# Moving the SBUF operands of a hybrid encoder layer from 64 and 192 to 0 modulo 256 bytes

## The chip, the cores and the metric

The kernel runs on one core of a Trainium2 chip. The metric is device time in microseconds, the median of three runs. Addresses in this document are byte offsets within a partition of SBUF, and the **phase** of an operand is the address of its first byte modulo 256.

## The reference, cut to what matters

One layer on 1,024 tokens of width 1,024, all in float32. `u = RMSNorm(x) @ W_in`; half of the columns go through a gated causal depthwise convolution of 31 taps, LayerNorm and swish; the others through chunk-causal retention with 4 heads of 128, per-head RMSNorm and a swish gate. Then

```python
x = x + concat([a_out, b_out], axis=-1) @ w_out     # 1024 x 1024
h = rms_norm(x, norm2_g)
x = x + square(relu(h @ w_ff1)) @ w_ff2              # 1024 x 4096 and 4096 x 1024
return rms_norm(x, final_g)
```

Neither the kernel before nor the change alters what is computed.

## The kernel before

**Matmuls.** A float32 product is made of three matmuls of type float32r, with both factors split into a high part and a low rest: `mm3` (L134 to L138) issues high by high (L136), high by low (L137) and low by high (L138) into one PSUM bank. The stationary operand (`lhsT`) is 128 columns of 4 bytes, the moving operand (`rhs`) 512 columns of 4 bytes (256 in four calls at the very end). Each matmul is preceded by the load of its stationary operand, which runs beside the matmul before it. There are 1,418 calls of `mm3`, so 4,254 such matmuls; 371 plain float32 ones (transposes, retention) come on top. In the rows the first name after the arrow is the moving operand and the second the stationary one.

**Stages, in the order of time.** Input projections and convolution (`acc<-cols,w` and `acc<-w,cols`), retention, the out-projection of the retention half and then of the convolution half (`out_proj`, L484; stationary `mh`, `ml`; 16 calls of 24 matmuls), the columns of the normed result (`normed_columns`, L605), the first feed-forward product, the second one (`ff2_group`, L845; `acc<-w,w` shown as `acc<-w`) and the last norm and stores. The first feed-forward product takes one pair of hidden blocks plainly (`plain_pair`, L727: `acc<-h,w1h`, 96 matmuls) and 15 pairs by Strassen's scheme with seven products of 12 matmuls each (`strassen_pair`, L741: M1, M2, M6, M5, M7, M3, M4, in that order; M1 and M2 are `pa<-h,w1h` and `pb<-h,w1h`). Between the plain pair and the first Strassen pair's third product stand sums of the stashed columns, which come back from DRAM (`bf`, L803, and the operations on VectorE and ScalarE from L806 to L820).

**Where the tiles lie.** Pools take their room one behind the other, in the order of L56 to L65, and a tile's slot is rounded up to 32 bytes. Every tile that a matmul reads begins at its slot's start plus a multiple of 512 bytes, so the slot decides the phase:

| pool | slots x bytes (before) | first address, phase before | phases of the slots before | phases after |
|---|---|---|---|---|
| `const` (ones, vectors, eight `r1` of 4 bytes) | small | 16,512 | mixed | mixed, 64 bytes shorter |
| `blkp` (`blk`) | 8 x 4,096 | 18,496, phase 64 | 64 | 0 |
| `wp` (`w`, `cols`, `h2`, `t`, `bf`, `w2raw`) | 13 x 8,192 | 51,264, phase 64 | 64 | 0 |
| `rawp` (`raw`, `xr` of the second product) | 2 x 4,096 | 157,760, phase 64 | 64 | 0 |
| `cp` (tag "c": `xcol`, `glu`, `y`, `xn`, `w1h`, `w1l`, `t12`, `t34`, `ysum`) | 7 x 4,224 | 165,952, phase 64 | 64, 192, 64, 192, 64, 192, 64 | 0 |
| `sp` (tag "s": `mh`, `ml`, `a22`, `hid`, `part`, `kT`, `qT`, `xr` of L504) | 11 x 2,048 | 195,520, phase 192 | 192 | 0 |
| `hx` (`tx`, the low part for M7) | 1 x 8,192 | 220,096, phase 192 | 192 | 0 |

The length of a `cp` slot comes from its longest tile, `glu` (L270): 30 columns of padding and 1,024 of data, 4,216 bytes, rounded to 4,224, which is 16 x 256 + 128. The slots of `cp` are handed out in turn, so from pair to pair the high and low parts of W1 (`w1h`, `w1l`, made in `split_pairs`, L667) come to lie at phase 64 or 192. Of the 4,254 float32r matmuls 3,150 have both operands at phase 64, 1,044 a moving operand at 64 and a stationary one at 192, 36 the reverse, and 24 both at 192.

For example, in the pair whose product M1 starts at 521.79 us, the four operands of M1 and M2 lie in slots of phase 192; in the pair whose M1 starts at 560.67 us they lie in slots of phase 64.

Of the kernel before, what the change touches and what calls it, by code (L numbers as in the profile page):

```python
# [8 lines left out]
F32 = mybir.dt.float32  # L9
# [6 lines left out]
P = 128  # L16
D = 1024
S = 1024
# [3 lines left out]
PAD = KT - 1  # L22
# [8 lines left out]
GB = 2  # L31
NG = NB // GB
WARM = 11
QUOTA = (4, 16, 11, 11, 13, 33, 22, 14)
NPAIR = NF // 2

# [2 lines left out]
def hybrid_layer_kernel(  # L39
# [16 lines left out]
    const = pool("const", 1)  # L56
# [3 lines left out]
    cp = pool("cp", 7)  # L60
# [87 lines left out]
    def mean_sq(src):  # L148

        tr = sp.tile([P, D], BF16, tag="s", name="trash")  # L150
        ss = tiny.tile([P, 1], F32, tag="ss1", name="ss")
        nc.scalar.activation(tr, src, AF.Square, scale=D**-0.5, accum_out=ss)
        return ss
# [60 lines left out]
                proj_tokens(w, b, a, d, d == 0, d == ND - 1)  # L214
        return accs

    r1 = {}

    def evac_v(b, acc):
        nc.vector.scalar_tensor_tensor(  # L220
# [18 lines left out]

    def stats(t):  # L240

        xt = cp.tile([P, D], F32, tag="c", name="xt")
        nc.sync.dma_start(xt, x[t * P : (t + 1) * P, :])
        r1[t] = const.tile([P, 1], F32, name=f"r1_{t}")
        m = tiny.tile([P, 1], F32, tag="nmr", name="m1")
        nc.gpsimd.tensor_tensor(m, mean_sq(xt), eps1, ALU.add)
        nc.gpsimd.tensor_tensor(r1[t], m, mhalf[:, 0:1], ALU.pow)
# [19 lines left out]
    glu, marks = [], []  # L267

    def glu_gate(accs):
        g = cp.tile([P, PAD + S], F32, tag="c", name="glu")  # L270
        nc.gpsimd.memset(g[:, 0:PAD], 0.0)
        for h in range(2):
            zg = sp.tile([P, HALF], F32, tag="s", name="zg")
            nc.vector.tensor_tensor(zg, accs[1][h], r1_row[h], ALU.mult)
            sg = sp.tile([P, HALF], F32, tag="s", name="sg")
            nc.scalar.activation(sg, zg, AF.Sigmoid)
            sr = sp.tile([P, HALF], F32, tag="s", name="sr")
            nc.gpsimd.tensor_tensor(sr, sg, r1_row[h], ALU.mult)
            nc.vector.tensor_tensor(g[:, PAD + h * HALF : PAD + (h + 1) * HALF], accs[0][h], sr, ALU.mult)
        glu.append(g)  # L280
        marks.append(len(pe_log))
# [17 lines left out]
    with tc.manual_schedule(engines=ordered):  # L299

        idle = pr.tile([P, 4, P], F32, tag="r", name="idle")
        for i in range(WARM):
            nc.tensor.matmul(idle[:, i % 4], lhsT=ones, rhs=ones, start=True, stop=True)
# [12 lines left out]
    for t in range(NB):  # L316
        stats(t)
# [16 lines left out]
    nc.sync.dma_start(trg, trig)  # L334

    glu_gate(first)
    wv = chunk_w(0)
    for q in range(2):
        accs[q].append(bank(1))
    for d in range(ND):  # L340
        glu_proj(w, 1, accs, d, 1)
    glu_gate(accs)

    def glu_tile(w, j):
# [14 lines left out]
    for j in range(2):  # L359
        if j == 1:  # L360
            wk = chunk_w(3)
        glu_gate(glu_tile(w, j))
# [213 lines left out]
    i = 0  # L576
    for (a, b), n in zip(zip(marks, marks[1:]), QUOTA):
        for j in range(n):
# [441 lines left out]
```

## Time and profile before

| | |
|---|---|
| median of 3 runs | 1077.8 us (1075.88 to 1078.59) |
| the profiled execution | 1076.53 us |
| its span, first to last instruction | 1074.8 us |
| mean granted TensorE clock | 0.991 |
| TensorE busy | 1039.7 us, 97% of the span |
| VectorE, ScalarE, GpSimd busy | 803.4, 381.5, 69.4 us |
| HBM | 125 GB/s over the span |

The profiled execution is 1.73 us longer than its span; that is launch and end, which no row shows. Busy time of TensorE counts each matmul to its modelled end, so neighbours overlap: what a matmul costs in a dense stretch is the distance from its start to the next one's, not its duration.

### The profile page before, as it was taken

The numbers are of one execution on the slowest core, as the hardware profiler recorded it, in microseconds if no ns is written. First come the engines' busy times: TensorE is split into PE (matmuls) and PEld (weight loads), VectorE is DVE, ScalarE is ACT, GpSimd is POOL, SyncE is SP. The second block draws the span as 40 slices with busy tenths as digits, with TensorE's granted clock in tenths as the row PEclk, the third lists the DMA queues.
The fourth block names the chain that finished last, engine by engine and source line by source line (L and its number), as shares of the span: only waits on it lengthen the run. The fifth ranks groups of instructions, "written<-read, shape, count | busy, mean of one in ns | idle before, by whom it ended". The sixth has DMA issues, their size and how long they took to land.

```text
span 1074.8 us, 12628 instructions
## 1 busy us (share of the span) xinstructions
PE 1039.7 (97%) x4772; PEld 856.7 (80%) x4772; DVE 803.4 (75%) x975; ACT 381.5 (35%) x601; POOL 69.4 (6%) x134
## 2 busy tenths in 40 slices
PE   9999999999999989969999999999999999999996
PEld 7888888888888777748888888887788888888885
DVE  5397769999796455687677676776998878777857
ACT  7511111144531465333232332322453333433423
POOL 0400110021000311000000000000000000000003
PEclk9999999999999999979999999999999999999998
DMA  9412011002241024615334444356546344253324
GB/s 357 166 40 79 26 53 59 21 14 66 92 140 63 1 59 155 219 68 176 138 135 169 138 161 138 133 185 213 199 143 250 117 176 164 95 186 103 92 78 156
DMA packets 55020, 134.88 MB, mean 126 GB/s; under 512 B 5424, under 2 KB 13744, under 8 KB 54576
## 3 DMA queue, kind: packets, MB, share of 16 engines
q1 hardware_dynamic: 54960, 134.09, 36.4%
q8 instruction: 37, 0.61, 0.2%
q14 instruction: 23, 0.19, 0.1%
HBM read 97.11 MB, written 36.96 MB: 125 GB/s over the span
## 4 chain that ended last, share of the span: by engine, by line
PE 52%; DVE 2%; DMA 1%; issue 1%; POOL 1%; ACT 0%; SPq 0%; POOLq 0%; DVEq 0%; ACTq 0%
PE acc L136 9%; PE acc L138 9%; PE acc L137 9%; PE pa L138 5%; PE pa L137 5%; PE pa L136 5%; PE pb L138 4%; PE pb L137 4%; PE pb L136 4%; DMA xr<-x1M 1%; DVE ot L917 0%; DMA w2raw<-in_w_dram 0%; DVE blk L909 0%; ACT trash L936 0%; POOL var L938 0%
## 5 line engine op out<-in xcount | busy, mean ns | idle before, releaser
L136 PE MATMUL acc<-w 128*128 128x512 f32 x454 | 176.8, 389 | 0.8 <-ACT w L187 0.8
L137 PE MATMUL acc<-w 128*128 128x512 f32 x454 | 176.2, 388 | 0.0
L138 PE MATMUL acc<-w 128*128 128x512 f32 x454 | 175.9, 388 | 0.0
L373 DVE SCALAR_TENSOR_TENSOR y<-glu,vec,y 128x1024 f32<-128x1024 f32 x120 | 153.7, 1290 | 2.0
L136 PEld LDWEIGHTS acc<-w 128*128 128x128 f32 x454 | 85.2, 188 | 19.8 <-ACT w L187 1.3
L136 PE MATMUL acc<-w,cols 128*128 128x512 f32 x256 | 100.1, 391 | 0.0
L137 PE MATMUL acc<-w,cols 128*128 128x512 f32 x256 | 99.8, 390 | 0.0
L138 PE MATMUL acc<-w,cols 128*128 128x512 f32 x256 | 99.8, 390 | 0.0
L137 PEld LDWEIGHTS acc<-w 128*128 128x128 f32 x454 | 85.2, 188 | 17.6
L138 PEld LDWEIGHTS acc<-w 128*128 128x128 f32 x454 | 85.2, 188 | 17.6
L187 ACT ACTIVATE w<-xr 128x1024 fp32r<-128x1024 f32 (+1 forms) x56 | 56.2, 1004 | 105.5 <-PE acc L138 57.4
L188 DVE TENSOR_TENSOR w<-xr,w 128x1024 fp32r<-128x1024 f32 (+1 forms) x56 | 64.7, 1155 | 27.9 <-ACT w L187 27.8
L889 DVE TENSOR_TENSOR blk<-acc,blk 128x512 f32<-128x512 f32 x112 | 72.7, 686 | 11.8 <-PE acc L138 11.6
L113 ACT ACTIVATE w<-raw 128x1024 fp32r<-128x1024 f32 (+1 forms) x36 | 34.8, 966 | 96.9 <-PE acc L138 71.6
L136 PE MATMUL pa<-t,w1h 128*128 128x512 f32 x120 | 47.9, 399 | 10.0 <-ACT part L751 10.0
L138 PEld LDWEIGHTS acc<-w,cols 128*128 128x128 f32 x256 | 48.1, 188 | 9.8
L137 PEld LDWEIGHTS acc<-w,cols 128*128 128x128 f32 x256 | 48.1, 188 | 9.8
L136 PEld LDWEIGHTS acc<-w,cols 128*128 128x128 f32 x256 | 48.1, 188 | 9.8
L136 PE MATMUL acc<-w,mh 128*128 128x512 f32 x128 | 52.0, 406 | 0.0
L187 ACT ACTIVATE w1h<-t 128x1024 fp32r<-128x1024 f32 x30 | 31.7, 1057 | 55.9 <-PE pb L138 55.9
L136 PE MATMUL acc<-cols,w 128*128 128x512 f32 x128 | 50.0, 392 | 1.1 <-ACT w L113 0.9
L137 PE MATMUL acc<-w,mh 128*128 128x512 f32 x128 | 50.7, 396 | 0.0
(193 smaller groups left out, 2094.6 us busy)
## 6 DMA issues: line engine op xcount, KB each, us to landing
raw<-in_w_dram SPq DMA_DIRECT2D x34, 512.0 KB, 3.6
w2raw<-in_w_dram SPq DMA_DIRECT2D x30, 512.0 KB, 4.5
raw<-in_w_in_dram SPq DMA_DIRECT2D x23, 512.0 KB, 3.3
xt<-in_x_dram SPq DMA_DIRECT2D x8, 512.0 KB, 9.0
raw<-in_w_out_dram SPq DMA_DIRECT2D x8, 512.0 KB, 3.3
xr<-in_x_dram SPq DMA_DIRECT2D x16, 256.0 KB, 3.0
stash<-full SPq DMA_DIRECT2D x16, 256.0 KB, 2.6
out_dram<-ot SPq DMA_DIRECT2D x16, 256.0 KB, 2.0
```

What stands on the lines that cost most here:

```text
L113: nc.scalar.activation(w[:, 0, i], raw[:, i], AF.Copy)
L136: nc.tensor.matmul(acc, lhsT=lh, rhs=rh, start=first, stop=False, **kw)
L137: nc.tensor.matmul(acc, lhsT=lh, rhs=rl, start=False, stop=False, **kw)
L138: pe_log.append(nc.tensor.matmul(acc, lhsT=ll, rhs=rh, start=False, stop=last, **kw))
L187: nc.scalar.activation(hi, src, AF.Copy)
L188: nc.vector.tensor_tensor(lo, src, hi.bitcast(F32), ALU.subtract)
L373: nc.vector.scalar_tensor_tensor(y, glu[c][:, k : k + S], tap(k), y, ALU.mult, ALU.add)
L889: nc.vector.tensor_tensor(t, acc[lane][r], t, ALU.add)
```

## The change

The tile `glu` becomes 4,352 bytes long (17 x 256), and with it each slot of `cp`. The eight `r1` tiles of the constants pool become six tiles of 8 bytes: tokens 0 and 1 share one, tokens 2 and 3 another. That frees two slots of 32 bytes, so `const` ends at 18,432 instead of 18,496, and every later pool begins 64 bytes further down. Together all operands of the 4,254 float32r matmuls come to lie at phase 0. `ones`, `ident`, `mhalf` and `vec` stay where they are.

```diff
+ALIGN = 256
...
-    r1 = {}
+    r1, r1_pair = {}, None
...
     def stats(t):
 
+        nonlocal r1_pair
         xt = cp.tile([P, D], F32, tag="c", name="xt")
         nc.sync.dma_start(xt, x[t * P : (t + 1) * P, :])
-        r1[t] = const.tile([P, 1], F32, name=f"r1_{t}")
+        if t % 2 == 0 or t >= 4:
+            r1_pair = const.tile([P, 2], F32, name=f"r1_{t}")
+            r1[t] = r1_pair[:, 0:1]
+        else:
+            r1[t] = r1_pair[:, 1:2]
...
     def glu_gate(accs):
-        g = cp.tile([P, PAD + S], F32, tag="c", name="glu")
+        g = cp.tile([P, S + ALIGN // 4], F32, tag="c", name="glu")
```

The instructions of all five engines, their order, their sizes and what each waits for are the same in both kernels; addresses alone differ, and two of the eight `r1` are now the second column of their tile.

## Rows read from the trace of the kernel before

**Rows 1.** The page's first part: busy time, share of the span, instructions
```profile
PE 1039.7 (97%) x4772; PEld 856.7 (80%) x4772; DVE 803.4 (75%) x975; ACT 381.5 (35%) x601; POOL 69.4 (6%) x134
```

**Rows 2.** Waits of TensorE: waiting instruction, releaser, total us, times, longest
```profile
PE pa L136 <- ACT part L751: 10.0, 1, 10.0
PE pt L617 <- DVE xn L608: 6.7, 8, 1.2
PE pa L138 <- DVE w1l L188: 2.3, 1, 2.3
```

**Rows 3.** Windows: stretch, its us, engines' busy us (x count), clock, DMA share, GB/s
```profile
474.50:751.80 277.30, 277.30 (x1201) 225.70 (x1200) 196.07 (x267) 83.84 (x114) 0.00 (x0) 1.00 0.45 156
763.00:1046.00 283.00, 283.00 (x1249) 233.97 (x1248) 225.16 (x255) 107.11 (x113) 0.19 (x1) 1.00 0.42 141
```

**Rows 4.** Timeline of TensorE, M1 and M2, slots at 192: start, duration
```profile
521.79 0.40 PE L136 MATMUL pa<-h,w1h 128*128 128x512 f32 x1
...
527.38 0.40 PE L136 MATMUL pa<-t,w1h 128*128 128x512 f32 x1
```

**Rows 5.** The same two products of a later pair, slots at 64
```profile
560.67 0.39 PE L136 MATMUL pa<-h,w1h 128*128 128x512 f32 x1
...
566.12 0.40 PE L136 MATMUL pa<-t,w1h 128*128 128x512 f32 x1
```

**Rows 6.** Timeline of TensorE, an out-projection of the retention half
```profile
314.63 0.39 PE L137 MATMUL acc<-w,mh 128*128 128x512 f32 x1
...
319.76 0.40 PE L138 MATMUL acc<-w,ml 128*128 128x512 f32 x1
```

**Rows 7.** Timeline of TensorE, half an out-projection of the convolution half
```profile
395.53 0.39 PE L137 MATMUL acc<-w,mh 128*128 128x512 f32 x1
...
397.84 0.39 PE L138 MATMUL acc<-w,ml 128*128 128x512 f32 x1
```

**Rows 8.** Timeline of TensorE, the plain pair
```profile
433.07 0.40 PE L136 MATMUL acc<-h,w1h 128*128 128x512 f32 x1
...
448.33 0.40 PE L137 MATMUL acc<-h,w1h 128*128 128x512 f32 x1
```

**Rows 9.** Timeline of TensorE, a piece of the last block, 256 columns wide
```profile
1064.14 0.28 PE L138 MATMUL acc<-w 128*128 128x256 f32 x1
...
1064.50 0.28 PE L138 MATMUL acc<-w 128*128 128x256 f32 x1
```

**Rows 10.** VectorE, ScalarE by tile `w1l`, `w1h`: ns min/median/max, first and last start
```profile
L188 DVE TENSOR_TENSOR w1l<-t,w1h x30: 1215/1219/1227, 467.3 to 734.4; 128x1024 fp32r<-128x1024 f32 x30
...
L187 ACT ACTIVATE w1h<-t x30: 1045/1056/1065, 449.6 to 732.8; 128x1024 fp32r<-128x1024 f32 x30
```

**Rows 11.** Timeline: TensorE behind its long wait
```profile
465.05 0.80 PE L136 MATMUL pa<-t,w1h 128*128 128x512 f32 x1 [10.01 <-ACT part L751]
...
469.15 0.63 PE L136 MATMUL pa<-t,w1h 128*128 128x512 f32 x1
469.58 0.63 PE L137 MATMUL pa<-t,w1h 128*128 128x512 f32 x1
...
471.69 0.40 PE L136 MATMUL pa<-t,w1h 128*128 128x512 f32 x1
```

**Rows 12.** The chain that ended last, 739 to 762 us: start, us, what
```profile
743.08 5.07 DMA w2raw<-in_w_dram
...
755.32 5.39 DMA xr<-x1M
...
761.84 0.50 PE acc L136
```

**Rows 13.** DMA issues by line: count, KB each, median us to landing
```profile
xr<-in_x_dram SPq DMA_DIRECT2D x16, 256.0 KB, 3.0
...
bf<-stash SPq DMA_DIRECT2D x3, 1024.0 KB, 5.8
...
xr<-x7M SPq DMA_DIRECT2D x7, 256.0 KB, 2.7
```

## The prediction

> **What bounds the kernel now.** I read the page's busy times first: TensorE is busy for 97% of the span [rows 1]. Next the waits of TensorE: beside one of 10.0 us, one of 2.3 us and eight short ones of 6.7 us together there is little [rows 2], so nearly all of the time is the matmuls following one another. Their own durations are modelled and overlap, so the third view is that of windows in which TensorE never pauses: the stretch divided by the count is what one matmul costs. In the second feed-forward product this is 283.00 / 1249 = 226.6 ns, in the Strassen pairs 277.30 / 1201 = 230.9 ns [rows 3], for the same matmul of 512 columns at the same granted clock of 1.00 (2.4 GHz).
>
> The fourth view is the timeline of two spots that differ in nothing but where the stationary operands lie. M1 and M2 of one pair, with their W1 parts in slots of phase 192, take 5.59 us for 24 starts, 232.9 ns each [rows 4]. The same two products of a later pair, with the parts in slots of phase 64, take 5.45 us, 227.1 ns each [rows 5]. Lines, moving tiles, pool and the work of the other engines are the same. So a float32r matmul whose two operands have different phases costs some 6 ns more than one whose operands agree. VectorE and ScalarE show nothing of the kind: their passes over the same rotating slots last 1215 to 1227 and 1045 to 1065 ns [rows 10], with not 2% between the shortest and the longest.
>
> Whether the sum of the phases or their difference decides, the rows tell only in part: agreement at phase 64 is seen in all of the second product, agreement at 192 in 24 matmuls alone, and at phase 0 nowhere.
>
> **The change part by part.** No instruction is added, removed or moved, on no engine and no queue; the two joined `r1` tiles are written and read by the same instructions with the same waits. Their price is nothing. What is left is the addresses: all 4,254 float32r matmuls get equal phases.
>
> *Strassen pairs.* 1,201 matmuls at 230.9 ns become matmuls at 226.6 ns [rows 3]: 1,201 x 4.3 ns = 5.2 us.
>
> *Out-projections.* Their stationary tiles all lie at 192 and their weights at 64. In the retention half 22 starts take 5.13 us, 233.2 ns each [rows 6]; in the convolution half 10 starts take 2.31 us, 231.0 ns each [rows 7]. 192 matmuls x 6.6 ns + 192 x 4.4 ns = 2.1 us.
>
> *Plain pair.* 66 starts in 15.26 us, 231.2 ns each [rows 8]; 96 x 4.6 ns = 0.4 us.
>
> *What of this is on the path.* The sum is 7.7 us. Two pieces don't count. Ahead of the wait of 10.0 us TensorE runs into sums that VectorE makes of tiles that come back from DRAM; the last plain matmul that this chain needs ends near 443 us, and the 46 matmuls after it only reach the wait earlier: 46 x 6.6 ns = 0.3 us. At the end of the Strassen pairs the chain leaves TensorE near 739 us for VectorE and two loads of 5.07 and 5.39 us and comes back at 761.84 us [rows 12]; the 53 matmuls from there to 751.9 us give 53 x 4.3 ns = 0.2 us that a load's end takes back. What is late next, in both places, is the load. **Net 7.2 us.**
>
> *Transfers.* Their ends in SBUF move from phase 64 or 192 to 0. The trace has no transfer at phase 0. Of equal size, loads into slots of phase 192 land in 3.0 us and into phase 64 in 2.7 us [rows 13], a tenth apart and not under equal load. On the chain lie two loads of 5.07 and 5.39 us [rows 12] and one of 5.8 us behind the plain pair [rows 13], 16.3 us: a tenth either way is 1.6 us. I take nothing, since the rows can't tell phase from load, and keep both ends for the range.
>
> *Clock.* Behind the wait of 10 us TensorE runs at half clock: starts are 0.43 us apart where 0.23 us is usual, from 465.05 to 471.69 us, about ten matmuls [rows 11], so 2 us. The wait stays and grows by 0.3 us. The low clock may end sooner or later against the program; between none and twice its cost that is 2 us either way. I take no change.
>
> *The matmuls that already agree.* Some 2,950 matmuls go from agreeing at 64 to agreeing at 0. The rows bound one from both sides: 226.6 ns is what agreement costs at 64, 232.9 ns what disagreement costs [rows 3, 4]; below, 512 columns cost 226.6 ns and 256 columns 0.36 us / 3 = 120 ns [rows 3, 9], so the columns alone take 106.6 ns per 256 and 13.4 ns are a constant that could fall. I take 226.6 ns, to which agreement at 64 is nearest, and leave the ends to rivals.
>
> **Sum.** 1076.5 - 7.2 = 1069.3 us for an execution like the profiled one. That one is 1.3 us under the median; from the median it would be 1070.6. I put the time between: **1070.0 us**.
>
> **The rivals.**
>
> *No change.* The 6 ns could come with the pools and what fills them, not with the phase: operands at 192 were all written by ScalarE and VectorE shortly before. Then nothing happens: 1075.9 to 1078.6 us, as the runs before. Against it stand rows 4 and 5, whose operands come from one pool and from the same writers. The Trainium skill sides with this rival: SBUF — State Buffer (Who interferes with whom) gives TensorE two independent read ports, one for the moving operand and one for the load of the stationary one, and says that TensorE waits for nobody; its section Operand start alignment speaks of legality and says that its runs timed nothing. By that page the sum would be zero. The trace disagrees with 232.9 against 227.1 ns [rows 4, 5]. I give it 0.11.
>
> *Every matmul gets faster.* The constant of 13.4 ns [rows 3, 9] could itself be a matter of beginning at phase 64, where both operands start and end inside a block of 128 bytes and touch one block more than at phase 0. Then 4,254 matmuls lose up to 13.4 ns, 57 us, and with the 7.2 us the time would be near 1012 us; a half of it gives 1041. For it: the constant is the same for 512 and 256 columns, as one extra block would be. Against it: the load of the stationary operand, equally constant, explains it as well. The Trainium skill, TensorE: Matmul & The Clock Gate (Back-to-back issue gap), gives N / 2.4 GHz + 2.5 ns, 216 ns for 512 columns; by that figure the estimate is 45 us off the matmuls that now take 226.6 ns. No row here shows a matmul of this kind at 216 ns. I give it 0.11.
>
> *Every matmul gets slower.* Agreement may be cheap because both operands begin in the middle of a block; beginning both on the edge of the same one, the two reads could collide as they now do at different phases. The place is the second feed-forward product and the input projections, some 2,950 matmuls that are undisturbed now; each would pay up to 6.3 ns (232.9 - 226.6), +18.6 us, and the disagreeing ones would gain nothing: 1095 us. It decides from 7.2 us / 4,254 = 1.7 ns per matmul upward; at 2.5 ns the kernel is slower by over 0.3%. Against it: phase 192 begins as far inside a block as 64 does, so no row speaks for or against an edge. I give it 0.07.
>
> **How the numbers follow.** The forecast has 0.71. Its own range is 1066 to 1073.5 us: the spread of the runs (1.4), transfers (1.6) and clock (2) on either side of 1070, not all at once. A measurement of this kernel tells about 0.3%, 3.2 us, from no change; the forecast's range lies beyond that. Faster: 0.71 + 0.11 = 0.82, less a little for a forecast that falls short, so 0.81. Same: 0.11 and that little, 0.12. Slower: 0.07. The range reaches from the forecast's lower end to the top of the no-change case, 1066 to 1078 us, and leaves the two large rivals out, 0.18.
>
> **What would show it.** In the trace of the changed kernel the window of the Strassen pairs should give 226.6 ns per matmul as the second product's does; M1 and M2 should take 5.44 us in every pair; out-projections 22 starts in 4.99 us; the waits of 10.0 and 2.3 us should stay. If the pairs stay at 230.9 ns, the phase was not the cause. If the second product leaves 226.6 ns in either direction, phase 0 differs from phase 64, and my forecast is wrong by 4.25 us per ns.

## The result and the profile after

The changed kernel takes **1070.34 us** (median; 1070.0 us was predicted, 1066 to 1078 the range), the kernel before 1078.12 us beside it. The ratio is 0.9931, with a 95% interval from 0.9911 to 0.995. Of the four executions of the changed kernel three took 1070.04 to 1070.44 us and one, at a mean granted clock of 0.556, took 1751.85 us: it counts in the median and not in the ratio. The profiled execution took 1070.04 us, its span is 1068.3 us (1074.8 before) and its mean granted clock 0.991 as before. Line numbers of the profile after stand 1 to 6 higher (L136 to L138 are now L137 to L139, L751 is L757).

The page's first part answers to [rows 1]. TensorE's busy time fell by 6.9 us; VectorE and ScalarE stayed within 1 us (803.4 and 381.5 before).

```profile
PE 1032.8 (97%) x4772; PEld 856.6 (80%) x4772; DVE 802.5 (75%) x975; ACT 381.5 (36%) x601; POOL 69.5 (7%) x134
```

The waits of TensorE, the same three as in [rows 2]:

```profile
PE pa L137 <- ACT part L757: 10.0, 1, 10.0
PE pt L623 <- DVE xn L614: 7.3, 8, 1.2
PE pa L139 <- DVE w1l L189: 2.3, 1, 2.3
```

The windows over the same 1,201 and 1,249 matmuls as [rows 3] (stretch, us, then busy us and count of PE, PEld, DVE, ACT, POOL, clock, DMA share, GB/s), and a third one over the half-clock stretch:

```profile
473.77:745.70 271.93, 271.93 (x1201) 225.27 (x1200) 195.00 (x267) 83.86 (x114) 0.00 (x0) 1.00 0.45 159
756.60:1039.55 282.95, 282.95 (x1249) 234.11 (x1248) 225.41 (x255) 107.22 (x113) 0.19 (x1) 1.00 0.42 141
463.70:470.50 6.80, 4.47 (x10) 3.11 (x11) 6.80 (x8) 2.94 (x3) 0.00 (x0) 0.50 0.22 77
```

The Strassen pairs went from 277.30 to 271.93 us, 226.4 ns per matmul. The second feed-forward product is where it was, 226.5 ns: whether both operands begin at 64 or both at 0 makes no difference. (The edges of a window cut a matmul, so its quotient is some 0.2 ns low; between two starts the steady matmul takes 226.7 ns.)

TensorE's timeline, at the places of [rows 6, 7, 8, 11, 4, 5], in order of time:

```profile
314.60 0.39 PE L138 MATMUL acc<-w,mh 128*128 128x512 f32 x1
...
317.14 0.39 PE L137 MATMUL acc<-w,mh 128*128 128x512 f32 x1
...
319.63 0.39 PE L139 MATMUL acc<-w,ml 128*128 128x512 f32 x1
...
394.79 0.40 PE L138 MATMUL acc<-w,mh 128*128 128x512 f32 x1
...
397.07 0.39 PE L139 MATMUL acc<-w,ml 128*128 128x512 f32 x1
...
432.29 0.39 PE L137 MATMUL acc<-h,w1h 128*128 128x512 f32 x1
...
447.25 0.39 PE L138 MATMUL acc<-h,w1h 128*128 128x512 f32 x1
...
463.74 0.79 PE L137 MATMUL pa<-t,w1h 128*128 128x512 f32 x1 [9.98 <-ACT part L757]
...
471.68 0.40 PE L139 MATMUL pb<-t,w1l 128*128 128x512 f32 x1
...
520.22 0.39 PE L137 MATMUL pa<-h,w1h 128*128 128x512 f32 x1
...
525.66 0.39 PE L137 MATMUL pa<-t,w1h 128*128 128x512 f32 x1
...
558.30 0.39 PE L137 MATMUL pa<-h,w1h 128*128 128x512 f32 x1
...
563.74 0.39 PE L137 MATMUL pa<-t,w1h 128*128 128x512 f32 x1
```

M1 and M2 take 5.44 us in the pair that had 5.59 and in the pair that had 5.45 [rows 4, 5]: the two are alike now. The plain pair's 66 starts take 14.96 us instead of 15.26 [rows 8], 226.7 ns each. The out-projection of the retention half is not uniform: 11 starts from 314.60 to 317.14 take 230.9 ns each, the next 11, to 319.63, 226.4 ns. Before, the 22 took 233.2 on average [rows 6]. This block begins behind four transposes, and TensorE needs about 11 matmuls to come to its steady pace. Read the same way, the starts of the other blocks of both out-projections come to it after 3 to 11.

The chain that ended last, at the place of [rows 12] (start, us, what):

```profile
737.17 4.98 DMA w2raw<-in_w_dram
...
749.32 5.03 DMA xr<-x1M
...
755.48 0.50 PE acc L137
```

The start of the same instruction in both timelines shows where the time came from:

| instruction | before, us | after, us | gain so far |
|---|---|---|---|
| first `pb<-diag,ones` between the out-projections' halves | 357.79 | 357.08 | 0.71 |
| last transpose of `xn`, in the plain pair (`pt`) | 431.26 | 430.47 | 0.79 |
| first matmul behind the wait of 10 us | 465.05 | 463.74 | 1.31 |
| first `pb<-t,w1h`, just behind the half-clock stretch | 472.62 | 471.92 | 0.70 |
| last matmul of the Strassen pairs | 751.86 | 745.75 | 6.11 |
| second product, behind the two loads | 763.13 | 756.74 | 6.39 |
| end of the span | 1074.8 | 1068.3 | 6.5 |

### The profile page after: what moved, and what is told of

Its sections match the earlier page's. It is cut to its first block, busy times and chain, and to the rows that moved or that the text cites. A ratio compares the mean times of both kernels' runs of the same rounds, so it can differ in the third digit from the quotient of the medians.

```text
span 1068.3 us, 12628 instructions
## 1 busy us (share of the span) xinstructions
PE 1032.8 (97%) x4772; PEld 856.6 (80%) x4772; DVE 802.5 (75%) x975; ACT 381.5 (36%) x601; POOL 69.5 (7%) x134
## 4 chain that ended last, share of the span: by engine, by line
PE 51%; DVE 2%; DMA 1%; issue 1%; POOL 1%; ACT 0%; SPq 0%; POOLq 0%; DVEq 0%; ACTq 0%
PE acc L137 9%; PE acc L139 9%; PE acc L138 9%; PE pa L139 5%; PE pa L137 5%; PE pa L138 5%; PE pb L137 4%; PE pb L138 4%; PE pb L139 4%; DVE ot L923 0%; DMA xr<-x1M 0%; DMA w2raw<-in_w_dram 0%; DVE blk L915 0%; ACT trash L942 0%; POOL var L944 0%
## 5 line engine op out<-in xcount | busy, mean ns | idle before, releaser
L137 PE MATMUL acc<-w 128*128 128x512 f32 x454 | 176.7, 389 | 0.5 <-ACT w L188 0.5
L138 PE MATMUL acc<-w 128*128 128x512 f32 x454 | 176.2, 388 | 0.0
L139 PE MATMUL acc<-w 128*128 128x512 f32 x454 | 175.8, 388 | 0.0
L137 PEld LDWEIGHTS acc<-w 128*128 128x128 f32 x454 | 85.2, 188 | 19.3 <-ACT w L188 0.9
L137 PE MATMUL acc<-w,cols 128*128 128x512 f32 x256 | 100.1, 391 | 0.0
L138 PE MATMUL acc<-w,cols 128*128 128x512 f32 x256 | 99.8, 390 | 0.0
L139 PE MATMUL acc<-w,cols 128*128 128x512 f32 x256 | 99.8, 390 | 0.0
L139 PEld LDWEIGHTS acc<-w 128*128 128x128 f32 x454 | 85.2, 188 | 17.7
L138 PEld LDWEIGHTS acc<-w 128*128 128x128 f32 x454 | 85.2, 188 | 17.4
L137 PE MATMUL pa<-t,w1h 128*128 128x512 f32 x120 | 47.8, 398 | 10.0 <-ACT part L757 10.0
L139 PEld LDWEIGHTS acc<-w,cols 128*128 128x128 f32 x256 | 48.1, 188 | 10.0
L137 PEld LDWEIGHTS acc<-w,cols 128*128 128x128 f32 x256 | 48.1, 188 | 9.9
L138 PEld LDWEIGHTS acc<-w,cols 128*128 128x128 f32 x256 | 48.1, 188 | 9.7
L137 PE MATMUL acc<-w,mh 128*128 128x512 f32 x128 | 51.6, 403 | 0.0
L137 PE MATMUL acc<-cols,w 128*128 128x512 f32 x128 | 50.0, 392 | 1.2 <-ACT w L114 0.9
L138 PE MATMUL acc<-w,mh 128*128 128x512 f32 x128 | 50.2, 392 | 0.0
```

The lines of the kernel that those rows point to most:

```text
L137: nc.tensor.matmul(acc, lhsT=lh, rhs=rh, start=first, stop=False, **kw)
L138: nc.tensor.matmul(acc, lhsT=lh, rhs=rl, start=False, stop=False, **kw)
L139: pe_log.append(nc.tensor.matmul(acc, lhsT=ll, rhs=rh, start=False, stop=last, **kw))
```

## The experiments

All times of the kernel before beside these runs lie between 1075.4 and 1079.63 us. A time that is given without a ratio is that of a single execution. The diffs are against the changed kernel and shortened to the lines that matter. Two operands of a matmul are called *in step* when their phases agree.

### The two parts of the change, each alone

Everything at 64 instead of 0 (long `cp` slots, `r1` as before):

```diff
-    r1_pair = const.tile([P, 2], F32, name=f"r1_{t}")
...
+    r1[t] = const.tile([P, 1], F32, name=f"r1_{t}")
```

> The tile glu keeps its 4,352 bytes, but the eight r1 tiles are separate again, so every operand of the 4,254 float32r matmuls lies at phase 64 instead of 0. If the difference of the two phases decides, nothing is lost: 226.7 ns per matmul in the Strassen pairs and 1070.3 us, as with the change. If both operands have to begin at phase 0, the Strassen pairs go back towards 231 ns and the time towards 1078 us, or the second feed-forward product leaves 226.7 ns.

The move down by 64 bytes without the longer slots:

```diff
-        g = cp.tile([P, S + ALIGN // 4], F32, tag="c", name="glu")
+        g = cp.tile([P, PAD + S], F32, tag="c", name="glu")
```

> Only the move by 64 bytes is made: wp, blkp and rawp at phase 0, cp alternating between 0 and 128, sp at 128; 3,150 matmuls have both operands at 0, 1,044 a stationary operand at 128. If the difference decides, this is the kernel before again: the Strassen pairs at 230.9 ns, 1078 us. If the start at phase 0 counted by itself, the 3,150 would gain and the time would lie under 1075 us.

Windows of the Strassen pairs and of the second product, first with all operands at 64:

```profile
474.50:750.00 275.50, 275.26 (x1215) 227.60 (x1214) 198.88 (x272) 85.14 (x116) 0.00 (x0) 1.00 0.46 161
757.00:1037.00 280.00, 280.00 (x1236) 231.64 (x1235) 223.56 (x252) 106.33 (x111) 0.00 (x0) 1.00 0.42 142
```

then with the move alone:

```profile
474.50:750.00 275.50, 275.50 (x1193) 224.12 (x1192) 194.72 (x265) 83.85 (x114) 0.00 (x0) 1.00 0.45 154
757.00:1037.00 280.00, 279.71 (x1233) 231.04 (x1233) 225.17 (x251) 108.87 (x113) 0.00 (x0) 1.00 0.44 149
```

All at 64: 1070.32 us, ratio 0.9932 (0.9918 to 0.9945), 226.7 ns per matmul in the pairs. The move alone: 1077.21 us, ratio 0.9996 (0.9987 to 1.0005), 230.9 ns. The longer slots bring the whole gain; "begin at 0 modulo 256" brings nothing beside "begin alike".

### A constant difference of 32 and of 64 bytes

An unused tile ahead of `cp` moves all its slots against the weights (N is 32 or 64):

```diff
+    gap = pool("gap", 1).tile([P, N // 4], F32, name="gap")
     cp = pool("cp", 7)
```

> The changed kernel with 32 unused bytes ahead of cp: cp, sp and hx move to phase 32, wp, blkp and rawp stay at 0, so 1,680 float32r matmuls have operands that differ by 32. If any difference costs what 128 costs, the Strassen pairs go to about 232 ns, above the kernel before since every W1 part disagrees now, and the time to about 1079 us. If only a difference of 128, half of the period, collides, they stay at 226.7 ns and 1070 us. If a small difference spreads the two reads better than none, they fall under 226.7 ns.

> As the kernel with 32 unused bytes, with 64: 1,680 float32r matmuls whose operands differ by 64. Any difference costs: about 232 ns in the Strassen pairs and 1079 us. Only half of the period costs: 226.7 ns and 1070 us. A difference spreads the reads: under 226.7 ns.

The same window of the pairs, at 32:

```profile
474.50:750.00 275.50, 275.50 (x1182) 221.85 (x1182) 192.53 (x263) 81.93 (x112) 0.00 (x0) 1.00 0.43 150
```

and at 64:

```profile
474.50:750.00 275.50, 275.50 (x1182) 221.97 (x1182) 193.34 (x265) 82.01 (x112) 0.00 (x0) 1.00 0.42 149
```

1078.99 and 1080.93 us, 233.1 ns per matmul over the window in both. In the pairs 32 bytes cost as much as 64.

### All weights out of step

The slots of the weight pool `wp`, whose phases were all alike, get 64 bytes each. To make room, the pool of the small norm factors (`tiny`) has four slots for each tag instead of eight:

```diff
-  tiny = pool("tiny", 8)
+  tiny = pool("tiny", 4)
...
-  wp.tile([P, 4, HALF], F32R, ...)
+  wp.tile([P, 4 * HALF + 16], F32R, ...)[:, 0 : 4 * HALF]
```

> The slots of the weight pool wp are lengthened from 8,192 to 8,256 bytes, so that the weights of the projections and of FF2 step by 64 bytes modulo 256 from slot to slot, and 892 of 4,254 matmuls keep operands that agree; the arithmetic and the order are those of the changed kernel. Theory (the difference decides for every matmul of the program, in FF2 as in the Strassen products): matmuls of FF2 at 231 to 233 ns where they were at 226.7; some 3,360 x 6 ns = 20 us more, about 1090 us. Rival (the loss belongs to the Strassen products and output projections, for instance to operands that VectorE has just written): FF2 at 226.7 ns as before, 1070 to 1073 us.

```profile
474.00:750.00 276.00, 276.00 (x1188) 223.75 (x1188) 196.39 (x269) 81.86 (x112) 0.00 (x0) 1.00 0.42 148
772.00:1053.00 281.00, 281.00 (x1217) 228.12 (x1216) 221.00 (x249) 103.74 (x109) 0.00 (x0) 1.00 0.42 140
```

1086.94 us, 16.6 us above the changed kernel where 20 were expected. The second product left 226.6 ns for 230.9. The waits of TensorE did not grow with the smaller `tiny` (the three of the list above are 9.8, 6.6 and 2.3 us). So the price is not peculiar to the pairs or to one pool: the matmuls of the second product pay it too when their addresses are put out of step. Who wrote the operands this run doesn't separate, since ScalarE and VectorE write them in both stages.

### Fifteen differences in one program

The W1 parts of each Strassen pair begin `off` elements of 4 bytes further on, another `off` for each pair (their slots have 256 bytes to spare); M4, with `a22`, stays in step between the pairs.

```diff
-  hi = cp.tile(list(raw.shape), F32R, tag="c", name="w1h")
+  hi = cp.tile([P, D + 64], F32R, tag="c", name="w1h")[:, off : off + D]
```

> In the changed kernel the stationary operands w1h and w1l of the 15 Strassen pairs 1 to 15 begin 4, 8, 16, 24, 32, 48, 64, 96, 128, 160, 192, 224, 240, 248 and 252 bytes behind a multiple of 256; a pair uses them in 72 matmuls (M1, M2, M6, M5, M7, M3), and M4, which takes a22, stays at a difference of 0. Theory (a matmul costs more whenever its two operands differ modulo 256): 226.7 ns at M4, and between 231 and 234 ns at all 15 differences, 15 x 72 x 6 ns = 6.5 us more than the changed kernel, about 1076.8 us. Rival A (only a difference of 32 bytes or more counts, nearer ones are free): 226.7 ns at 4, 8, 16, 24, 240, 248 and 252 bytes, 8 x 72 x 6 ns = 3.5 us more, about 1073.8 us. Rival B (0 is not the best difference, some other one is faster): at least one pair whose 72 matmuls stand less than 226 ns apart.

Windows from the first start of a pair's 72 matmuls to the start behind them, at 8, 16, 24, 32, 128, 192, 240 and 248 bytes (the count has one more, which began before):

```profile
482.98:499.59 16.61, 16.61 (x73) 13.53 (x72) 11.20 (x17) 4.82 (x7) 0.00 (x0) 1.00 0.47 163
502.31:518.63 16.32, 16.32 (x73) 13.52 (x72) 11.20 (x17) 4.81 (x7) 0.00 (x0) 1.00 0.47 166
521.36:537.99 16.63, 16.63 (x73) 13.50 (x72) 11.20 (x17) 4.81 (x7) 0.00 (x0) 1.00 0.47 163
540.73:557.52 16.79, 16.79 (x73) 13.52 (x72) 11.16 (x17) 4.81 (x7) 0.00 (x0) 1.00 0.45 163
...
618.94:635.69 16.75, 16.75 (x73) 13.57 (x72) 11.21 (x17) 4.81 (x7) 0.00 (x0) 1.00 0.45 164
...
658.02:674.50 16.48, 16.48 (x73) 13.52 (x72) 11.21 (x17) 4.81 (x7) 0.00 (x0) 1.00 0.48 165
...
696.74:713.06 16.32, 16.32 (x73) 13.52 (x72) 11.20 (x17) 4.81 (x7) 0.00 (x0) 1.00 0.46 165
715.79:732.58 16.79, 16.79 (x73) 13.52 (x72) 11.21 (x17) 4.81 (x7) 0.00 (x0) 1.00 0.44 163
```

Divided by 72: 230.7 ns at 8, **226.7 at 16**, 231.0 at 24, 233.2 at 32, 232.6 at 128, 228.9 at 192, **226.7 at 240**, 233.2 at 248; at 252, too, the matmuls stand 226.7 ns apart up to the last wait of the pairs. The time was 1076.11 us. No theory had this. "Any difference costs" fails at 16, 240 and 252; "near ones are free" fails at 8, 24 and 248; nothing is below 226.7. A new theory was needed: every pair but the first came out of M4, whose operands agree and whose last starts stood at the fast pace again, so a difference may *keep* a pace that it would not *find*.

### The same scan in another order, and groups with a fresh start

> The scan again with other steps in another order: w1h and w1l of the Strassen pairs 1 to 15 begin 252, 4, 12, 20, 28, 236, 244, 256, 16, 8, 248, 232, 208, 176 and 4 bytes behind a multiple of 256. In the first scan 16, 240 and 252 bytes stood at 226.7 ns, 4 bytes at 232.9, 8 at 230.7, 248 at 233.3; its pair 1 (4 bytes) came out of the half-clock stretch, all others out of 12 matmuls with agreeing operands at 226.7 ns. Theory A (the difference alone sets the price, 4 and 252 are not alike): 252 in pair 1 at 226.7, 4 in pairs 2 and 15 at 232.9, 16 at 226.7, 8 at 230.7, 248 at 233.3. Theory B (a near difference keeps a rhythm of 226.7 that it finds running, and doesn't find it by itself): 252 in pair 1 over 230, 4 in pairs 2 and 15 at 226.7. 256 is 226.7 by both; over 230 there would say that not the phase but the offset counts. Time: about 1075 us by either.

Pair 1 of this run, at 252 bytes throughout, has two windows: 24 matmuls behind the plain pair (in step), and, in the same pair and the same slots, the 34 behind the half-clock stretch. Then the pairs at 4, 12, 20 and 256:

```profile
448.15:453.59 5.44, 5.44 (x26) 4.50 (x25) 5.41 (x7) 2.16 (x3) 0.00 (x0) 1.00 0.71 256
471.80:479.73 7.93, 7.93 (x35) 6.38 (x34) 3.31 (x5) 2.14 (x3) 0.00 (x0) 1.00 0.34 113
482.46:499.20 16.74, 16.74 (x73) 13.50 (x72) 11.20 (x17) 4.81 (x7) 0.00 (x0) 1.00 0.47 163
501.95:518.27 16.32, 16.32 (x73) 13.52 (x72) 11.20 (x17) 4.82 (x7) 0.00 (x0) 1.00 0.47 167
520.99:537.78 16.79, 16.79 (x73) 13.52 (x72) 11.20 (x17) 4.81 (x7) 0.00 (x0) 1.00 0.47 162
...
597.99:614.31 16.32, 16.32 (x73) 13.51 (x72) 11.20 (x17) 4.81 (x7) 0.00 (x0) 1.00 0.47 166
```

The 252-byte pair ran at 5.44 us / 24 = 226.7 ns before the interruption and at 7.93 / 34 = 233.2 ns after it. The difference of its operands stayed what it was; only the products were others. In the first scan the same products (M6, M5 and M7) at 252 bytes, without an interruption, ran at 8.16 us / 36 = 226.7 ns:

```profile
740.77:748.93 8.16, 8.16 (x37) 6.76 (x36) 2.35 (x3) 2.17 (x4) 0.00 (x0) 1.00 0.95 286
```

So theory A, the difference alone, is out. Theory B holds for 252 and 16 (226.7 again), and for 12, 28 and 244 (16.32 us as well), but not for 4, 20 and 236, which lost the pace they came in with (232.5, 233.2 and 231.7). 8 and 248 repeated 230.7 and 233.3. 256 bytes is 226.7: the phase counts, not the offset. The time was 1073.4 us.

The other run starts each group afresh (`d` counts elements of 4 bytes):

```diff
+  for d in (0, 1, 2, 4, 8, 16, 32, 48, 60, 62, 63, 0):
+    for i in range(28):
+      n, c0 = (P if i < 4 else HALF), d + (i % 6) * P
+      nc.tensor.matmul(tail[:, :n], lhsT=x[0][:, 0, 0, c0 : c0 + P], rhs=w[0][:, 0, 0, :n], ...)
```

> Ahead of the last FF2 products stand 12 groups of 28 matmuls whose results nobody reads: 4 of 128 moving columns, which break the rhythm as the transposes do, then 24 of 512 columns with 128 stationary ones. The stationary operand begins 0, 4, 8, 16, 32, 64, 128, 192, 240, 248, 252 and again 0 bytes behind a multiple of 256, the moving one at 0. Theory (agreeing operands find the rhythm of 226.7 ns from any start; others don't): both groups at 0 reach 226.7 after 2 to 12 matmuls and keep it; 32, 64, 128 and 248 stay between 231 and 234 on average to the end of their 24. Open: 4, 16, 240 and 252, which stand at 226.7 in the first scan or not; at 226.7 by the end of the 24 if a near difference finds the rhythm by itself, over 230 if it only keeps it. Rival (the price is not of the addresses but of Strassen's operands, which VectorE and ScalarE have just written, beside traffic of theirs): all 12 groups at 226.7. The time grows by 12 x (4 x 60 + 24 x 230) ns = 69 us, to 1139 us.

Windows over 15 of a group's last 16 matmuls, at 0, 4, 16, 240, 252 and again 0 bytes:

```profile
1040.02:1043.42 3.40, 3.40 (x16) 2.82 (x15) 0.00 (x0) 0.00 (x0) 0.00 (x0) 1.00 0.00 0
1045.97:1049.46 3.49, 3.49 (x16) 2.81 (x15) 0.00 (x0) 0.00 (x0) 0.00 (x0) 1.00 0.00 0
...
1057.98:1061.47 3.49, 3.49 (x16) 2.83 (x15) 0.00 (x0) 0.00 (x0) 0.00 (x0) 1.00 0.02 5
...
1088.03:1091.46 3.43, 3.43 (x16) 2.81 (x15) 0.00 (x0) 0.00 (x0) 0.00 (x0) 1.00 0.02 5
...
1100.05:1103.55 3.50, 3.50 (x16) 2.82 (x15) 0.00 (x0) 0.00 (x0) 0.00 (x0) 1.00 0.00 0
1106.09:1109.49 3.40, 3.40 (x16) 2.82 (x15) 0.00 (x0) 0.00 (x0) 0.00 (x0) 1.00 0.00 0
```

Both groups at 0 find 226.7 ns (3.40 / 15); all ten others stay above it: 232.7 at 4 and 16, 228.7 at 240, 233.3 at 252, and 3.43 to 3.50 us for the 15 at 8, 32, 64, 128, 192 and 248. VectorE and ScalarE are idle in these rows and the DMA queues nearly so, so the rival of traffic is out too; and the same two tiles serve all twelve groups, so it is not who wrote them. 16 and 252, which kept the pace in the scans, don't find it here. The time was 1143.8 us, 5 above the sum: the narrow matmuls cost about 100 ns each, where 60 were assumed, and the first wide one behind them about 285.

### What the constant of 13.4 ns is

```diff
+  for n, cols, reps in ((128, 512, 30), (64, 512, 24), (32, 512, 24), (128, 256, 24)):
+    for i in range(reps):
+      nc.tensor.matmul(tail[:n, :cols], lhsT=x[0][:, 0, 0, (i % 8) * P : (i % 8) * P + n], rhs=w[0][:, 0, 0, :cols], ...)
```

> Ahead of the last FF2 products stand 102 more matmuls whose results nobody reads: 30 of a 128-column stationary operand and 512 moving columns, 24 of a 64-column, 24 of a 32-column stationary operand with 512 moving columns, and 24 of 128 columns with 256 moving ones, all at a difference of 0. 512 columns at 2.4 GHz are 213.3 ns, and the steady matmul of the changed kernel takes 226.7 ns, 13.4 ns more. Theory (the load of the next stationary operand takes its time from the stream of the moving one, in proportion to its columns): 226.7, 220.0 and 216.7 ns. Rival (a constant per matmul, whatever is loaded): 226.7 ns in all three groups. The group of 256 columns: 120 ns by both. The time grows by 78 x 225 ns + 24 x 120 ns = 20.4 us, to about 1090.8 us.

```profile
1037.36:1044.16 6.80, 6.80 (x32) 5.58 (x31) 0.89 (x2) 0.00 (x0) 0.00 (x0) 1.00 0.00 0
1044.16:1049.67 5.51, 5.51 (x25) 3.19 (x24) 0.00 (x0) 0.00 (x0) 0.00 (x0) 1.00 0.00 0
1049.67:1055.24 5.57, 5.57 (x26) 2.70 (x25) 0.00 (x0) 0.00 (x0) 0.00 (x0) 1.00 0.00 0
1055.24:1058.12 2.88, 2.88 (x26) 2.88 (x24) 0.00 (x0) 0.00 (x0) 0.00 (x0) 1.00 0.00 0
```

6.80 / 30 = 226.7 ns with 128 stationary columns, 5.51 / 24 = 229.6 with 64, 5.57 / 24 = 232.1 with 32, and 120.0 for 256 moving columns; 1092.21 us. Both theories fell: a smaller load gains nothing, and in fact the steady pace is lost, to the end of both groups, although the operands agree. The loads themselves did get shorter (PEld 3.19 and 2.70 us for 24, against 5.58 for 30). What sets 13.4 ns stays open.

### The identity in step as well

The vectors move ahead of `ones` and `ident`:

```diff
+    vec = const.tile([P, NV], F32, name="vec")
     ones, ident
```

> The vectors of the layer norms are allocated ahead of the identity, so that the identity and the ones also begin at 0 modulo 256; all else stands where the changed kernel has it. Theory 1 (the slow first matmuls after each batch of transposes in the output projections come from the transposes' own operands, which differ by 64 bytes or so from the identity): the output projections reach 226.7 ns sooner, up to 0.6 us less, 1069.7 us. Theory 2 (they come from the change of operation, whatever the addresses): 1070.3 us, as the changed kernel.

It took 1071.44 us (1070.61 to 1072.87; ratio 0.9948, 0.9935 to 0.9962), no better than the changed kernel. In its trace the first, third and fifth block of the retention half do settle sooner, after 6 matmuls instead of 10 or 11, and later ones do not; by 357 us that is worth 0.03 us, and a clock drop costs 1.5 us right behind it. The window there, of this kernel:

```profile
361.40:364.30 2.90, 2.90 (x13) 2.71 (x13) 0.88 (x2) 0.60 (x1) 0.58 (x2) 0.53 0.00 0
```

and of the changed kernel:

```profile
361.30:364.20 2.90, 2.90 (x19) 2.55 (x18) 0.88 (x2) 0.60 (x1) 1.03 (x3) 1.00 0.01 3
```

At a granted clock of 0.53 (1.2 GHz for nearly all of it) 13 matmuls pass where 19 do at 1.00. TensorE had come from a row of narrow matmuls with pauses in both kernels. Why the clock fell in one alone isn't settled; the run can't tell whether the move of `ident` or of `ones` matters. Neither this nor any other version tried is faster than the changed kernel.

## Why the prediction was right, and where its terms were off

**The cause** was right: the pairs fell to the second product's cost, M1 and M2 take the predicted 5.44 us in every pair, and the waits of 10.0 and 2.3 us stayed. The runs at 32 and 64 bytes and with the weights out of step show that it is the addresses, and the run with all operands at 64 that the difference decides, and not where both begin. What the prediction took for a price of each matmul is a pace, which TensorE finds some matmuls behind an interruption; how the chip makes it is not shown.

**Strassen pairs:** 5.2 us predicted, 5.4 measured (0.70 to 6.11 in the table). **Plain pair:** 15.26 to 14.96 us for 66 starts, 4.5 ns each against the 4.6 predicted.

**Out-projections:** this is the mis-sized term, 2.1 us predicted, 0.8 measured (the table's second line). The working gave all 384 matmuls the steady cost from the first on. In the retention half the first 3 to 11 matmuls behind each batch of transposes are still slow (230.9 ns for 11 in the block of the rows); 22 starts went from 5.13 to 5.03 us, where 4.99 had been named as the sign: 0.10 us a block and not 0.145. In the convolution half the 10 starts of [rows 7] went from 2.31 to 2.28 us, and most of what the matmuls gained there was given back: between the table's first two lines the gain grows only from 0.71 to 0.79 us, and the eight waits for `xn` grew from 6.7 [rows 2] to 7.3 us. That VectorE's chain to `xn` did not get shorter by as much as TensorE came earlier is how I read this; no run takes it apart. The prediction named what is late next at two other places, and not here.

**Lost ahead of the wait of 10 us:** 0.3 us predicted, nothing measured; the wait is 9.98 where it was 10.01 [rows 11], so the loads and sums it waits for came earlier with the rest.

**Clock:** no change taken, 2 us either way in the range. Behind the wait the first matmul of ordinary length (0.40 us) now starts at 471.68 us, 7.9 us behind 463.74; before, it was 6.6 us, from 465.05 to 471.69 [rows 11]. That costs 0.6 us (1.31 to 0.70 in the table), inside the bounds. The change is not shown to be its cause: the two kernels with extra matmuls ahead of the last products are the changed kernel up to that place, and there the first start at full pace came 9.1 and 9.5 us behind the wait, against 7.9 in the changed kernel and 7.4 in the second scan. So executions alone differ by more than the 0.6 us.

**End of the pairs:** a loss of 0.2 us predicted, a gain of 0.3 measured. The two loads on the chain took 4.98 and 5.03 us where they had taken 5.07 and 5.39 [rows 12]. One execution doesn't tell whether phase 0 or less traffic made them shorter.

Together, 5.4 + 0.8 + 0.5 (to the wait) - 0.6 + 0.3 = 6.4 us of the 6.5, against 7.2 predicted. The errors went both ways, and the time came out 0.3 us from the forecast partly by that, and partly by luck in the starting point: an execution like the profiled one was forecast at 1069.3 us and took 1070.04; the choice of 1070.0, between 1069.3 and 1070.6, made up for the 0.7 us by which the gain fell short of 7.2.

**A count:** the second product has 1,362 float32r matmuls and the input projections 1,152, together 2,514, where the prediction has some 2,950 for matmuls that already agree. Its rival *every matmul slower* would have cost 2,514 x 6.3 ns = 15.8 us by that, near 1092 us and not 1095; the forecast takes nothing from this count.

**The rivals.** *No change* is out: the interval of the ratio ends at 0.995. The Trainium skill, SBUF — State Buffer (Who interferes with whom), which gives TensorE two independent read ports and says that it waits for nobody, would have made all these runs alike; 226.7 against 233 ns for the same matmul at another address (the windows at all-64 and at a difference of 32) disagrees. *Every matmul faster* is out: no window gives less than 226.4 ns for 512 columns, not even with a quarter of the stationary ones. The figure of 216 ns for 512 columns, which the Trainium skill, TensorE: Matmul & The Clock Gate (Back-to-back issue gap), gives for the gap of an isolated matmul, was seen in no run here. *Every matmul slower* is out: the second product is at 226.5 ns at phase 0.

## What to carry to other kernels

Where TensorE is busy without a pause, divide windows by counts: two stages of the same matmul at different costs are a finding, and the timeline of one stage at two times shows what they don't share. Here it was worth lengthening a slot by 128 bytes so that every slot a matmul reads begins alike modulo 256; whether all of them begin at 0 or at 64 made no difference, and of the ten other differences tried from a fresh start none found the fast pace by itself. A per-matmul saving is worth less in short runs: count the matmuls behind each interruption apart, and ask for each short wait on another engine whether it takes the saving back.

## What the runs showed that was not expected

- The cost is not a fixed price per difference but a pace that TensorE settles into. With 128 stationary and 512 moving columns in step it reached 226.7 ns from every start looked at, within 3 to 11 matmuls. Out of step it settled, from a fresh start, between 228.7 and 233.3 ns at all ten differences tried.
- A pace once found can outlast the condition: at 252 bytes the same pair ran at 226.7 ns, and at 233.2 after an interruption. 12, 16, 28, 240 and 244 bytes kept it through 72 matmuls; 4, 8, 20, 24, 236, 248 and all eleven tried from 32 to 232 did not. No rule in these numbers was found.
- In step is not enough for narrower stationary operands: 229.6 ns at 64 columns and 232.1 at 32, slower than 226.7 at 128.
- VectorE and ScalarE felt nothing of it: their busy times moved by 0.9 us of 803 and by nothing of 381.5.
